# A hybrid DeltaNet and diffusion layer: a written TensorE order for the projections and the DeltaNet pairs, and two modulation blocks as float32 products

## The chip, the cores and the metric

The kernel runs on one core of a Trainium2 chip. The metric is the device time of one execution in microseconds (us); where several runs are compared, it is their median. Engines are named as follows: TensorE (PE in the rows, PEld its weight loads), VectorE (DVE), ScalarE (ACT), GpSimd (POOL), and SyncE (SP), which issues most transfers. All matrices are float32; a product of two of them is made of three one-pass products of a high and a low part (h and l in the tile names), unless the text calls it a float32 product.

## What is computed

One layer of a network for 128 context and 512 latent tokens (640 in all, width 1024). The reference, cut to the part that the change touches:

```python
def layer(x, mod, s0, ...):
    sh1, sc1, gt1, sh2, sc2, gt2 = jnp.split(mod[:, None, :], 6, axis=-1)   # mod = silu(c) @ w_mod + b_mod
    h = rms_norm(x, norm_gains[0]) * (1 + sc1) + sh1
    y, s_fin = mixing(h, s0, ...)
    x = x + gt1 * rms_norm(y, norm_gains[1])
    h = rms_norm(x, norm_gains[2]) * (1 + sc2) + sh2                         # the two blocks sh2, sc2
    gate, up = jnp.split(h @ w_ffn_in, 2, axis=-1)
    ...
def mixing(h, s0, ...):
    p = h @ w_in                                        # 45 tiles of 128 columns
    qkv, z, beta, a, sc, gates = jnp.split(p, SPLITS, axis=-1)
    qkv = jax.nn.silu(conv_centred(qkv, conv_qkv, n_rows))
    o_f, s_f = gated_delta_chunked(q, k, v, beta[0], g[0], s0[:, 0])         # and backwards
    ...
def gated_delta_chunked(q, k, v, beta, g, s0):          # chunks of 64 tokens
    lower = jnp.where(tri_strict, jnp.einsum('bhncd,bhned->bhnce', kb, k) * decay, 0.0)
    tmat = lax.linalg.triangular_solve(eye + lower, ...)                     # 64x64 per chunk and head
    ...
    def step(s, xs):                                    # the scan over the chunks
        v_new = u_c - jnp.einsum('bhcd,bhde->bhce', w_c, s)
        o = jnp.einsum('bhcd,bhde->bhce', q_c, s) + jnp.einsum('bhce,bhed->bhcd', a_c, v_new)
        s = s * jnp.exp(gl)[..., None, None] + jnp.einsum('bhcd,bhce->bhde', k_c, v_new)
        return s, o
```

## The kernel before, in words

The layer runs in stages: norm and modulation of the input, which gives hT (channels on partitions, all 640 tokens in one row); the projections of hT with the 45 tiles of w_in, with the DeltaNet beside them; the merge of the two branches; the output product; the feed-forward part. The change lies in the second of these stages.

A projection tile is 128 columns of w_in. `load_w` fetches its 512 KB into a wr buffer (two of them), ScalarE and VectorE split it into wh and wl in two halves, and `gemm_cm` multiplies it with one half of the tokens (320 columns): 24 products, three for each of eight blocks of the inner dimension, into one of three PSUM buffers named d. Each half is then taken out by ScalarE or VectorE. The tiles belong to q, k and v of four head pairs (`qkv`, with a convolution of three taps on VectorE and a Silu), to the gate z (`zgate`), to the short convolution branch (`short`, three tiles each) and to the merge gates (`gate_th`).

For each head pair, `prepare` turns q, k and v into token-major form (transposes on TensorE), normalises them, multiplies keys with keys and queries (the K products, from kqT), and solves a unit triangle: Md is transposed by 32x32 blocks on VectorE into blk, 30 steps of two instructions (otmp, then X) invert 128 blocks of 32 rows at once, and two transposes give RT and R. TensorE's products with RT and em give Y, and those of R and Y the rest of the 64x64 inverse. Then the tiles KU, RS, AQ and kt are filled for `scan`, which runs eight steps over the chunks, both directions and heads at once; each step is a few small products (EW, then KU) and two copies of the state into RS. Output products (AQ) and five transposes end a pair.

Every engine runs its instructions in the order in which they stand in the program. A scheduler set this order before: each instruction has a priority from its place in the code, raised within `high_priority` (state steps of `scan` by 300000, evacuations by 400000, splits by 200000, `prepare` by 1000), and the scheduler deals them out by its own estimate of when each can start. Buffers are given out in turn; an instruction that writes a buffer waits until the last reader of what was in it has ended.

The modulation blocks sh2 and sc2 are made on VectorE by `row_job`: for each of eight blocks of 128 input channels, w_mod (512 KB) is multiplied by one number per partition and added to a row sum gacc, once for each of the two conditioning vectors; then `cm_rows` splits the sum, adds it over the partitions with TensorE (a product with ones) and carries the row through DRAM into channel-major form.

## Time and profile before

| what | value |
|---|---|
| median of 3 runs | 1090.03 us (1087.43 to 1094.59) |
| profiled execution, its own time | 1085.44 us |
| its span, first to last instruction | 1083.7 us |
| mean granted TensorE clock in it | 0.981 of 2.4 GHz |
| TensorE busy | 1019.8 us, 94% |
| VectorE busy | 836.9 us, 77% |
| ScalarE busy | 483.2 us, 45% |
| GpSimd busy | 141.9 us, 13% |

The span is the profiled execution as the rows below see it; about 2 us of the execution lie outside it. Busy time is the time in which an engine has at least one instruction in work; products overlap, so a busy TensorE need not be at its peak.

### The profile page before, as it was taken

The page shows a single profiled execution, that of the slowest core. Times are in us where ns is not written, and L with a number is a line of the kernel's source. Part 1 is how long each engine was busy: PE and PEld are TensorE (multiplying, and loading weights), DVE is VectorE, ACT ScalarE, POOL GpSimd, SP SyncE. Part 2 cuts the span into 40 slices and gives each one's busy share as a digit, 9 for nine tenths or more (in the row PEclk, how much of TensorE's full clock was granted, in tenths as well). Part 3 has the DMA queues.
Part 4 walks back from the last instruction along what each step waited for, and adds up shares of the span by engine and source line. Part 5 has one row for each costly group of instructions (what it writes and reads, how often), then busy time and mean ns, then how long its engine had stood idle before and what let it go on. Part 6 is the DMA issues. An engine that isn't in the chain of part 4 may idle for free.

```text
span 1083.7 us, 19694 instructions
## 1 busy us (share of the span) xinstructions
PE 1019.8 (94%) x7729; PEld 925.9 (85%) x7729; DVE 836.9 (77%) x1698; ACT 483.2 (45%) x927; POOL 141.9 (13%) x168
## 2 busy tenths in 40 slices
PE   6999988988988989999998998999999999999997
PEld 3699987878887788899996887999999999788885
DVE  5767997897898888895895789888777775975336
ACT  5568436415525323434223476444445444624321
POOL 2215321153063050101000000000000000000000
PEclk9999989998999999999999998999999999999999
DMA  9335712163282374557853532323222322552214
GB/s 346 144 91 136 205 60 75 57 138 107 62 188 89 99 179 166 173 166 241 309 183 116 180 113 88 104 86 98 93 79 78 98 83 74 176 171 99 79 39 156
DMA packets 47399, 141.52 MB, mean 131 GB/s; under 512 B 9517, under 2 KB 10034, under 8 KB 47306
## 3 DMA queue, kind: packets, MB, share of 16 engines
q1 hardware_dynamic: 42746, 127.10, 35.9%
q0 software_dynamic: 4560, 13.15, 5.6%
q8 instruction: 61, 1.00, 0.4%
q14 instruction: 32, 0.26, 0.1%
HBM read 117.57 MB, written 12.18 MB: 120 GB/s over the span
## 4 chain that ended last, share of the span: by engine, by line
PE 63%; DVE 18%; DMA 3%; ACT 2%; issue 2%; SPq 1%; POOL 0%; DVEq 0%; ACTq 0%; POOLq 0%
PE acc L1166 21%; PE d L85 6%; PE d L83 6%; PE d L84 6%; PE acc L84 5%; PE acc L83 5%; PE acc L85 5%; PE d L1166 3%; DVE X L561 3%; DVE otmp L559 2%; PE s L643 2%; DVE wl L58 2%; PE v L614 1%; PE v L673 1%; DVE RT L565 1%
## 5 line engine op out<-in xcount | busy, mean ns | idle before, releaser
L83 PE MATMUL d<-hT,wh 128*128 128x320 f32 x720 | 228.4, 318 | 1.8 <-DVE cy L724 1.8
L85 PE MATMUL d<-hT,wl 128*128 128x320 f32 x720 | 228.9, 318 | 0.4 <-DVE wl L58 0.4
L84 PE MATMUL d<-hT,wh 128*128 128x320 f32 x720 | 227.2, 316 | 0.0
L57 ACT CAST wh<-wr 128x512 fp32r<-128x512 f32 x150 | 88.1, 620 | 155.1 <-PE d L84 90.4
L83 PEld LDWEIGHTS d<-hT,wh 128*128 128x128 f32 x720 | 137.3, 191 | 4.3 <-DVE cy L724 2.1
L85 PEld LDWEIGHTS d<-hT,wl 128*128 128x128 f32 x720 | 137.3, 191 | 4.2 <-issue 1.2
L84 PEld LDWEIGHTS d<-hT,wh 128*128 128x128 f32 x720 | 137.5, 191 | 2.0 <-issue 0.3
L58 DVE TENSOR_TENSOR wl<-wr,wh 128x512 fp32r<-128x512 f32 x150 | 103.1, 709 | 44.3 <-ACT wh L57 43.5
L1166 PE MATMUL acc<-mh,wl 128*128 128x320 f32 x280 | 86.9, 310 | 1.8 <-DVE wl L1101 1.8
L83 PE MATMUL acc<-wh,as 128*128 128x512 f32 x220 | 85.7, 390 | 2.1 <-ACT as L1300 2.1
L1166 PE MATMUL acc<-mh,wh 128*128 128x320 f32 x280 | 87.0, 311 | 0.3 <-ACT early L1180 0.3
L1166 PE MATMUL acc<-ml,wh 128*128 128x320 f32 x280 | 86.7, 310 | 0.0
L84 PE MATMUL acc<-wl,as 128*128 128x512 f32 x220 | 85.6, 389 | 0.0
L85 PE MATMUL acc<-wh,as 128*128 128x512 f32 x220 | 85.5, 389 | 0.0
L196 DVE SCALAR_TENSOR_TENSOR gacc<-wr,cv,gacc 128x1024 f32<-128x1024 f32 x64 | 80.7, 1280 | 4.0 <-DMA wr<-in_w_mod_dram 3.7
L1105 ACT CAST wh<-wr 128x512 fp32r<-128x512 f32 x66 | 40.7, 623 | 71.6 <-PE acc L1166 36.9
L1105 ACT CAST wh<-S 128x512 fp32r<-128x512 f32 x88 | 54.3, 621 | 36.3 <-PE d L1166 19.6
L1101 DVE TENSOR_TENSOR wl<-S,wh 128x512 fp32r<-128x512 f32 x88 | 60.2, 688 | 3.8 <-ACT wh L1105 2.9
L1101 DVE TENSOR_TENSOR wl<-wr,wh 128x512 fp32r<-128x512 f32 x66 | 45.4, 690 | 19.1 <-ACT wh L1105 18.1
L1166 PEld LDWEIGHTS acc<-mh,wl 128*128 128x128 f32 x280 | 52.8, 189 | 2.1 <-DVE wl L1101 2.0
L1166 PEld LDWEIGHTS acc<-mh,wh 128*128 128x128 f32 x280 | 52.7, 188 | 0.6 <-ACT early L1180 0.6
L1166 PEld LDWEIGHTS acc<-ml,wh 128*128 128x128 f32 x280 | 52.8, 189 | 0.0
(365 smaller groups left out, 2344.0 us busy)
## 6 DMA issues: line engine op xcount, KB each, us to landing
wr<-in_w_ffn_in_dram SPq DMA_DIRECT2D x48, 512.0 KB
wr<-in_w_in_dram SPq DMA_DIRECT2D x45, 512.0 KB
wr<-in_w_mod_dram SPq DMA_DIRECT2D x32, 512.0 KB
wr<-in_w_ffn_out_dram SPq DMA_DIRECT2D x22, 512.0 KB
mr<-in_w_mod_dram SPq DMA_DIRECT2D x16, 512.0 KB
thd<-gt SPq DMA_DIRECT2D x16, 320.0 KB
bth<-thd SPq DMA_DIRECT2D x16, 320.0 KB
wr<-in_w_br_dram SPq DMA_DIRECT2D x8, 512.0 KB
```

Of the source, the lines that this page charges most:

```text
L57: (high or nc.scalar.copy)(out=hi[:, s], in_=raw[:, s])
L58: (low or nc.vector).tensor_tensor(out=lo[:, s], in0=raw[:, s], in1=hi[:, s].bitcast(F32), op=ALU.subtract)
L83: mm(out, lhsT=ah, rhs=bh, start=start, stop=False)
L84: mm(out, lhsT=ah, rhs=bl, start=False, stop=False)
L85: mm(out, lhsT=al, rhs=bh, start=False, stop=stop)
L196: nc.vector.scalar_tensor_tensor(out=acc[v], in0=w, scalar=self.cv[:, k, v:v + 1], in1=acc[v], op0=ALU.mult, op1=ALU.add)
L559: nc.vector.tensor_tensor(out=t, in0=B[:, j + 1:32, j:j + 1].broadcast_to([P, n, j]), in1=X[:, j:j + 1, 0:j].broadcast_to([P, n, j]), op=A ...
L561: nc.vector.tensor_tensor(out=X[:, j + 1:32, 0:j], in0=X[:, j + 1:32, 0:j], in1=t, op=ALU.subtract)
L643: mm(ps[half(c2), o:o + 64], lhsT=w(d, c2, t, hd), rhs=R[:, d, c2, t, hd, :], start=True, stop=True)
L1101: tt = lambda o, a, b, op: nc.vector.tensor_tensor(out=o, in0=a, in1=b, op=op)
L1105: nc.scalar.copy(out=dst[0], in_=src)
L1166: nc.tensor.matmul(ps, lhsT=A[x][:, k], rhs=B[y][:, k], start=start and k == 0 and n == 0, stop=k == 3 and n == 2, skip_group_check=True)
```

## The change

Inside the stage, TensorE's instructions are no longer placed by the scheduler: within `manual_schedule` they stand as the code issues them. The other engines are still scheduled. The code is cut into steps with `yield`. `jobs` lists the projection tiles and, as two jobs "m", the modulation blocks 3 and 4 (sh2 and sc2); each step of a job is a quarter of a projection tile (half the inner dimension of one token half, 12 products) or, for "m", two float32 products of a 128x512 piece of w_mod. After each step, two chains are offered a turn: all of `scan` and all of `prepare`, for the four pairs one after the other. What a chain yields is how many turns it lets pass before its next step; a condition beside it holds the count until it is true.

`prepare` is put in another order (em, ea and qtT are fetched at its start, the tiles KU, RS and AQ are filled after the solve and only once the scan of the pair before has issued its output products), `mod_job` replaces `row_job` and `cm_rows` for two blocks, and some copies move from VectorE to ScalarE. Cut to its core:

```diff
+    def gemm_steps(self, w, xT, half):
+        sl = slice(half * HALF, (half + 1) * HALF)
+        ps = self.psd.tile([P, 512], F32, name="d", tag="d")[:, 0:HALF]
+        for k in range(KT):
+            self.mm3(ps, w[0][:, k, :], w[1][:, k, :], xT[0][:, k, sl], xT[1][:, k, sl],
+                     k == 0, k == KT - 1)
+            if k == KT // 2 - 1:
+                yield
         return ps
...
+    def mod_job(self, blk, out):
+        for h in range(2):
+            hs = slice(h * 512, (h + 1) * 512)
+            row = self.da.tile([5, 512], F32, name="mrow")
+            nc.sync.dma_start(out=row[4:5, :], in_=self.I["b_mod"][blk, :, hs])
+            ps = self.psd.tile([P, 512], F32, name="d", tag="d")
+            for kk in range(KT // 2):
+                w = self.wpool.tile([P, 2, 512], F32, name="wr", tag="wr")
+                nc.sync.dma_start(out=w, in_=self.I["w_mod"][blk - 2, 2 * kk:2 * kk + 2, :, hs].rearrange("k p c -> p k c"))
                 for i in range(2):
+                    k = 2 * kk + i
+                    nc.tensor.matmul(ps[0:4, :], lhsT=self.cz[:, k, :], rhs=w[:, i], start=k == 0, stop=k == KT - 1)
+                if kk == KT // 2 - 1:
+                    with self.urgent():
+                        nc.scalar.copy(out=row[0:4, :], in_=ps[0:4, :])
                 yield
+            self.cm_finish(out)(h, row)
...
+    def prepare(self, p, scanned):
...
         for j in (1, 0, 2):
+            yield 2 if j == 1 else 1, lambda: (p, j) in self.cm
...
+        for j, x in enumerate((kh, qh)):
+            yield 5 - 4 * j
...
         for ts in (slice(0, 4), slice(4, 5)):
+            yield 2
...
         for c2, b, s in quad:
-            cp = (nc.vector.tensor_copy, nc.scalar.copy)[b]
-            cp(out=Md[s, 0:20], in_=emv[s, :, b * 32:b * 32 + 32])
+            nc.scalar.copy(out=Md[s, 0:20], in_=emv[s, :, b * 32:b * 32 + 32])
...
+        yield 16
+        pw = self.psw.tile([P, 1024], F32, name="w", tag="w")
         Y = dn.tile([P, 20, 32], F32, name="Y")
...
+        yield 1, lambda: scanned() >= p
...
+        yield 2
+        pw = self.psw.tile([P, 1024], F32, name="w", tag="w")
         quads = [(c2, slice(c2 * 64, c2 * 64 + 32), slice(c2 * 64 + 32, c2 * 64 + 64)) for c2 in range(2)]
...
+    def scan(self, p):
+        yield 4, lambda: p in self.pre
...
-        cp = (nc.scalar.copy, nc.vector.tensor_copy)
+        cp = (nc.scalar.copy, nc.scalar.copy)
         for s_ in range(8):
...
+            yield 1
             if s_ == 7:
                 continue
...
+        self.scans = p + 1
+        yield 5
...
-        self.da = Tags(da, {"t25": 4})
+        self.da = Tags(da, {"t25": 2})
...
+        job = {"q": self.qkv, "z": self.zgate, "s": self.short, "g": self.gate_th,
+               "m": lambda blk, hT: self.mod_job(blk, cm[("sh2", "sc2")[blk - 3]])}
+        qkv = lambda p: [("q", p, j) for j in (1, 0, 2)]
+        jobs = (qkv(0) + [("z", 0), ("g", 0), ("s", 0)] + qkv(1) + [("z", 1), ("m", 3), ("g", 1), ("g", 2)]
+                + qkv(2) + [("z", 2), ("m", 4), ("s", 1)] + qkv(3) + [("z", 3), ("g", 3), ("g", 4), ("s", 2), ("g", 5)]
+                + [("s", 3)] + [("g", i) for i in range(6, 16)])
...
+            def tick(c):
+                if c.ready and not c.ready():
+                    return
+                c.ready = None
+                c.wait -= 1
+                if c.wait <= 0:
+                    c.step()
...
+        with tc.manual_schedule(engines={mybir.EngineType.PE}):
+            scan = Chain((x for p in range(NPAIR) for x in self.scan(p)), 300000)
+            prep = Chain((x for p in range(NPAIR) for x in self.prepare(p, lambda: self.scans)), 1000)
+            running = (x for n, *i in jobs for x in job[n](*i, hT))
+            used = 0
+            while not (scan.done and prep.done):
+                used += next(running, 1) is None
+                scan.tick()
+                prep.tick()
+            for _ in running:
+                pass
...
-        fill = itertools.chain(*(self.row_job(blk, rows2(mb), raws(mb, 4), self.cm_rows(cm[n], mb, ma, parts))
-                                 for blk, n in ((3, "sh2"), (4, "sc2"))))
-        steps = lambda n: [next(fill, None) for _ in range(n)]
-        self.gate_th(3, hT)
-        steps(2)
```

Three places of the order show it. In the rows, the d products with hT and wh or wl are projection products, w with kqT the K products, w or v with RT and em the first products that read the solved triangle.

TensorE, pair 0, from the last K product to the first product with RT; the new program, where 192 projection products stand between the two:

```order
L504 MATMUL w<-kqT 64x128 x4
L83 MATMUL d<-hT_75,wh 128x320
L84 MATMUL d<-hT_76,wh 128x320
L85 MATMUL d<-hT_75,wl 128x320
...
L542 MATMUL w<-RT,em 32x32 x40
```

The program before, where 255 stand there:

```order
L532 MATMUL w<-kqT 64x128 x4
L85 MATMUL d<-hT_75,wl 128x320
L83 MATMUL d<-hT_75,wh 128x320
L84 MATMUL d<-hT_76,wh 128x320
...
L578 MATMUL v<-RT,em 32x32 x40
```

So 63 projection products have left this place for later ones; in the new program the first product with RT comes after exactly four tiles.

VectorE, pair 0, the head of the triangular solve (blk, X and otmp are its tiles; wl is a split of a weight tile, bv and ss belong to the next pair's keys and values); before:

```order
L549 COPY Md<-em 32x640 x2
L553 STREAM_TRANSPOSE blk<-Md 128x32x32
L554 TENSOR_SCALAR X<-blk 128x1024
L555 MEMSET X 128x32
L559 TENSOR_TENSOR otmp<-blk,X 128x30
L561 TENSOR_TENSOR X<-X,otmp 128x30
L559 TENSOR_TENSOR otmp<-blk,X 128x58
L561 TENSOR_TENSOR X<-X,otmp 128x29x2
L559 TENSOR_TENSOR otmp<-blk,X 128x84
L58 TENSOR_TENSOR wl<-wr,wh 128x512 x2
L561 TENSOR_TENSOR X<-X,otmp 128x28x3
L468 TENSOR_TENSOR bv<-tk,beta 128x640
```

And now:

```order
L520 STREAM_TRANSPOSE blk<-Md 128x32x32
L58 TENSOR_TENSOR wl<-wr,wh 128x512 x2
L521 TENSOR_SCALAR X<-blk 128x1024
L522 MEMSET X 128x32
L526 TENSOR_TENSOR otmp<-blk,X 128x30
L528 TENSOR_TENSOR X<-X,otmp 128x30
L526 TENSOR_TENSOR otmp<-blk,X 128x58
L528 TENSOR_TENSOR X<-X,otmp 128x29x2
L730 TENSOR_TENSOR cx<-cx,d 128x320
L526 TENSOR_TENSOR otmp<-blk,X 128x84
L528 TENSOR_TENSOR X<-X,otmp 128x28x3
```

The copies of Md have gone to ScalarE, and the steps of the next pair's keys and values to a later place; splits and steps of the projections stand between those of the solve, as before.

TensorE, the stretch between RT of pair 0 and the last K product of pair 1, where the scan of pair 0 begins; before:

```order
L643 MATMUL s<-RS,EW 64x64
L83 MATMUL d<-hT_75,wh 128x320
L84 MATMUL d<-hT_76,wh 128x320
L85 MATMUL d<-hT_75,wl 128x320
L614 MATMUL v<-EW,kt 64x64 x20
L83 MATMUL d<-hT_75,wh 128x320
L84 MATMUL d<-hT_76,wh 128x320
L532 MATMUL w<-kqT 64x128 x4
```

And now (d with wr and cz are the float32 products of the modulation block, d with selb and mrow its row transposes):

```order
L178 MATMUL d<-wr,cz 4x512 x2
L651 MATMUL s<-RS,EW 64x64 x8
L178 MATMUL d<-wr,cz 4x512 x2
L651 MATMUL s<-RS,KU 64x64 x8
L487 MATMUL w<-ident,kh 128x128 x5
L178 MATMUL d<-wr,cz 4x512 x2
L651 MATMUL s<-RS,EW 64x64 x8
L487 MATMUL w<-ident,tk 128x128 x5
L178 MATMUL d<-wr,cz 4x512 x2
L651 MATMUL s<-RS,KU 64x64 x8
L192 MATMUL d<-selb,mrow 128x2 x4
```

Where projection products stood between the scan steps, two float32 products stand now, each pair of them on a freshly loaded piece of w_mod.

## Rows read from the trace of the kernel before

**Rows 1.** The page: busy time, share of the span and instructions of each engine.

```profile
PE 1019.8 (94%) x7729; PEld 925.9 (85%) x7729; DVE 836.9 (77%) x1698; ACT 483.2 (45%) x927; POOL 141.9 (13%) x168
```

**Rows 2.** Windows: length, busy time and instructions by engine, clock, DMA share, GB/s.

```profile
42.30:116.50 74.20, 71.63 (x542) 68.60 (x543) 54.72 (x120) 51.99 (x82) 28.95 (x29) 1.00 0.46 119
116.50:164.90 48.40, 42.34 (x285) 41.30 (x280) 46.55 (x117) 20.07 (x34) 11.36 (x10) 0.93 0.42 122
184.70:246.70 62.00, 54.62 (x510) 48.52 (x507) 57.24 (x147) 20.95 (x45) 17.98 (x23) 0.97 0.42 104
276.40:330.80 54.40, 47.66 (x436) 43.17 (x432) 50.84 (x140) 18.76 (x41) 18.91 (x23) 1.00 0.56 135
357.40:403.40 46.00, 41.41 (x387) 36.63 (x379) 40.89 (x108) 13.31 (x33) 16.45 (x22) 0.96 0.52 124
403.40:515.60 112.20, 110.66 (x1089) 103.05 (x1090) 88.45 (x125) 45.51 (x93) 9.51 (x12) 1.00 0.59 192
sum 397.20, PE 368.32 PEld 341.27 DVE 338.68 ACT 170.59 POOL 103.16; mean PE 61.39 PEld 56.88 DVE 56.45 ACT 28.43 POOL 17.19
```

**Rows 3.** The same windows, only instructions that touch hT.

```profile
42.30:116.50 74.20, 63.85 (x410) 60.14 (x409) 3.69 (x5) 4.49 (x8) 1.00 0.46 119
116.50:164.90 48.40, 39.97 (x255) 38.80 (x255) 0.00 (x0) 0.00 (x0) 0.93 0.42 122
184.70:246.70 62.00, 42.09 (x246) 36.27 (x246) 0.00 (x0) 0.00 (x0) 0.97 0.42 104
276.40:330.80 54.40, 38.33 (x233) 34.30 (x233) 0.00 (x0) 0.00 (x0) 1.00 0.56 135
357.40:403.40 46.00, 33.20 (x190) 28.79 (x190) 0.00 (x0) 0.00 (x0) 0.96 0.52 124
403.40:515.60 112.20, 94.94 (x594) 88.33 (x594) 0.00 (x0) 0.00 (x0) 1.00 0.59 192
```

**Rows 4.** Windows between RT and the next K, their sum.

```profile
sum 76.10, PE 69.45 PEld 63.08 DVE 57.22 ACT 47.98 POOL 21.90; mean PE 23.15 PEld 21.03 DVE 19.07 ACT 15.99 POOL 7.30
```

**Rows 5.** Waits of TensorE in the stage: total, times, longest.

```profile
PE v L578 <- DVE RT L565: 6.0, 4, 2.3
```

**Rows 6.** Timeline of TensorE, first stage: start, length, instruction.

```profile
33.54 5.31 PE L790 MATMUL m<-mr,cz 128*4 128x512 f32 x12
...
39.12 1.05 PE L180 MATMUL n<-selb,mrow 5*128 5x2 f32 x8
```

**Rows 7.** Timeline of TensorE, two projection products in a row.

```profile
272.90 0.31 PE L83 MATMUL d<-hT,wh 128*128 128x320 f32 x1
273.05 0.31 PE L84 MATMUL d<-hT,wh 128*128 128x320 f32 x1
```

**Rows 8.** Groups of VectorE in the stage: busy us, mean ns, idle before.

```profile
L58 DVE TENSOR_TENSOR wl<-wr,wh 128x512 fp32r<-128x512 f32 x92 | 65.1, 721 | 17.8 <-ACT wh L57 17.2
L561 DVE TENSOR_TENSOR X<-X,otmp 128x30 f32<-128x30 f32 (+14 forms) x120 | 47.8, 398 | 2.2
L559 DVE TENSOR_TENSOR otmp<-blk,X 128x30 f32<-128x30 f32 (+14 forms) x120 | 45.6, 380 | 2.4
L196 DVE SCALAR_TENSOR_TENSOR gacc<-wr,cv,gacc 128x1024 f32<-128x1024 f32 x34 | 42.9, 1278 | 0.1
L379 DVE SCALAR_TENSOR_TENSOR cm<-d,taps,cm 128x315 f32<-128x315 f32 x24 | 13.0, 541 | 9.4 <-ACT cm L401 9.3
...
L565 DVE STREAM_TRANSPOSE RT<-X 128x1024 f32<-128x1024 f32 x4 | 7.8, 1941 | 0.1
```

**Rows 9.** Groups of ScalarE in the stage.

```profile
L549 ACT COPY Md<-em 32x640 f32<-32x640 f32 x8 | 5.8, 726 | 2.3 <-DVE em L537 2.2
```

**Rows 10.** Timeline of VectorE, inside the solve of pair 1.

```profile
224.81 0.39 DVE L559 TENSOR_TENSOR otmp<-blk,X 128x228 f32<-128x228 f32 x1
225.11 0.17 DVE L679 TENSOR_SCALAR so<-so 128x10 f32<-128x10 f32 x1
```

**Rows 11.** Chain that ended last, near the scan of pair 1.

```profile
253.46 4.59 DMA wr<-in_w_in_dram
```

More of the change, by code (lines that the diff above doesn't have):

```diff
@@ L416, in prepare @@
+        half = lambda c2: slice(c2 * 64, c2 * 64 + 64)
+        qtT = dn.tile([P, 2, TOK], F32, name="qtT")
+        for hd in range(2):
+            nc.sync.dma_start(out=qtT[half(hd)], in_=g["scre"][:, 2 * p + hd].unsqueeze(0).broadcast_to([64, 2, TOK]))
         tok = {}
+        ss = dn.tile([P, 2, NT * 2], F32, name="ss")
         for j in (1, 0, 2):
+            yield 2 if j == 1 else 1, lambda: (p, j) in self.cm
+            cm = self.cm.pop((p, j))
             pw = self.psw.tile([P, 1024], F32, name="w", tag="w")
@@ L441, in prepare @@
+        qh, k, v = (tok[j] for j in range(3))
         fac = dn.tile([P, 2, 2, NT, 2], F32, name="fac")
@@ new lines, in prepare @@
+        nc.scalar.activation(out=em, in_=em, func=AF.Exp)
+        nc.scalar.activation(out=ea, in_=ea, func=AF.Exp)
+        kqT = dn.tile([P, 2, TOK], F32, name="kqT", tag="kb")
+        for j, x in enumerate((kh, qh)):
+            yield 5 - 4 * j
+            pw = self.psw.tile([P, 1024], F32, name="w", tag="w")
+            for t in range(NT):
+                nc.tensor.transpose(pw[:, t * P:(t + 1) * P], x[:, t * P:(t + 1) * P], self.ident)
+            nc.scalar.copy(out=kqT[:, j, :], in_=pw[:, 0:TOK])
@@ new lines, in prepare @@
+        RT = dn.tile([P, 32, 32], F32, name="RT", tag="kb")
+        R = dn.tile([P, 32, 32], F32, name="R")
+        nc.vector.transpose(out=RT.rearrange("p m x -> p x m"), in_=X)
+        nc.vector.transpose(out=R.rearrange("p m x -> p x m"), in_=X.rearrange("q r x -> q x r"))
+        yield 16
+        pw = self.psw.tile([P, 1024], F32, name="w", tag="w")
+        Y = dn.tile([P, 20, 32], F32, name="Y")
+        for m in range(20):
+            for c2 in range(2):
+                s0 = slice(c2 * 64, c2 * 64 + 32)
+                s1 = slice(c2 * 64 + 32, c2 * 64 + 64)
+                mm(pw[s0, m * 32:m * 32 + 32], lhsT=emv[s1, m, 0:32], rhs=RT[s1, m, :], start=True, stop=True,
+                   tile_position=(c2 * 64 + 32, c2 * 64))
@@ L899, in run @@
[L899 to L914 removed]
+        self.pre, self.cm, self.scans = {}, {}, 0
@@ new lines, in run, with __init__, step @@
+        class Chain:
+            def __init__(c, gen, offset):
+                c.gen, c.offset = gen, offset
+                c.step()
+            def step(c):
+                with tc.high_priority(offset=c.offset):
+                    w = next(c.gen, None)
+                c.wait, c.ready = (1 << 30, None) if w is None else w if isinstance(w, tuple) else (w, None)
+                c.done = w is None
+            def tick(c):
[4 more added lines that the diff above has]
+                if c.wait <= 0:
+                    c.step()
```

343 lines of the change are left out of this document (115 added, 228 removed).

## Prediction

> **What bounds the kernel now.** I read the page first. TensorE is busy for 94% of the span, VectorE for 77% [rows 1]; that is an average, and the change touches one stage, the 473 us in which TensorE multiplies the normalised input hT with 45 weight tiles and carries the DeltaNet work of four head pairs beside it. So I cut this stage into windows at two TensorE instructions of each pair p: the last key-query product of prepare (K for short) and the first product that reads the solved triangle RT. Between K and RT lies the triangular solve, 60 dependent VectorE steps, and TensorE cannot pass RT until it is done.
>
> The windows [rows 2] are, in this order: the start up to K of pair 0; K to RT of pairs 0, 1, 2, 3; RT of pair 3 to the end. The same windows for instructions that touch hT [rows 3] have as their PE count the number of projection products in each; the three stretches from one pair's RT to the next pair's K are added up [rows 4]. Two things are to be seen. In the four solve windows VectorE is busy 46.6 of 48.4, 57.2 of 62.0, 50.8 of 54.4 and 40.9 of 46.0 us: these 210.8 us go at VectorE's pace, and what TensorE does there (255, 246, 233 and 190 projection products) is filling. Outside them VectorE is busy 57 of 76 us between the pairs and 88 of 112 at the end, where TensorE is busy 69 and 111: these go at TensorE's pace. TensorE's idle time in the whole stage is small, 28.9 us in the six windows and 6.6 in the three; the wait for RT, 6.0 us in four times, is the one that a solve ends [rows 5].
>
> **Units.** One projection product starts 0.147 us after the one before [rows 7], so a quarter tile of twelve is 1.76 us. A float32 product of a 128x512 block on four rows counts as two in the trace; twelve of them took 5.31 us, so one whole product costs 0.885 us, and four small transposes of a modulation row 1.05 us [rows 6].
>
> **The change, part by part.** The stage's work on TensorE hardly shrinks. Added are 32 float32 products (28.3 us) and four times 1.05 us; removed are sixteen one-pass sums of 512 columns, by that pitch 0.235 us each, 3.8 us. Net +29 us. Removed from VectorE are 32 steps of 1.28 us on gacc [rows 8] with eight splits of their sums, and all state copies of scan and half those of Md go to ScalarE. The gacc steps stand in the last window, where TensorE is the one that is late: taking them off gives nothing by itself. So the question is whether the written order fills TensorE better. I go through the windows as the new order sets them.
>
> Start to K of pair 0: 312 products stand there instead of 410, 45.7 us instead of 60.1. The rest of TensorE's time, 74.2 less 60.1 less 2.6 idle, is 11.5 us and stays. New are waits: the transposes of q and of v of pair 0 stand directly behind their own last product, with ScalarE's tap and two VectorE taps of the convolution (0.54 us each [rows 8]), the Silu and the semaphores between. I take 3 us for each and 1 for gates; nothing and 14 us are the ends. 64 us, so 10 less.
>
> K to RT: now 192, 180, 192 and 192 products stand there, 168 fewer in all. The chain is VectorE's. First a lead: the last products with em and four copies of Md, now all on ScalarE at 0.73 us [rows 9] (two of four were on VectorE), 3.9 us. Then VectorE's own row of instructions from the transpose blk up to RT, which I counted in the new order: 92, 97, 102 and 96 instructions. In each 60 are the solve (30 at 0.380, 30 at 0.398: 23.3 us) and 8 are splits of the four weight tiles that TensorE needs meanwhile (5.8 us), the two big transposes at either end are 2.0 each, and the rest convolution, normalisation and short-branch steps; at the mean of their form they add up to 43.8, 42.7, 45.7 and 43.1 us. The form means [rows 8] contain the few steps that GpSimd held up. They overstate in one way: a short step starts before the one ahead has ended (the 0.39 us step at 224.81 has 0.09 us left when the next starts [rows 10]). I take 93% of the lists, 163 us, and four leads, 178.6 us; between 85% and 100% lie 165 and 191. That is 32 less than 210.8. TensorE's own work there is 28 us for pair 0 and about 37 for each other pair (27 us of products, the last scan steps, the output products, in pairs 1 and 2 the end of a modulation block), so it will stand at RT for about 16 us in pair 0 and 7 to 9 in each other, some 40 us where 6.0 are now.
>
> The Trainium skill, VectorE: DVE Perf Modes, in The DRAIN you can't avoid, says that the next VectorE instruction does not start until the pipe of the one ahead is empty. By that the lists count in full, 191 us, and the sum below would be 12 us more. That overlap speaks against it for these short steps, so I keep 93%.
>
> RT to the next K: 120, 108 and 216 products, 444 where 232 stand now, 65.0 us. 30 of the 32 float32 products are here with two of the four row transposes: 28.7 us. The small products of the pairs: in the windows K to RT and RT to K together TensorE now spends 286.9 us, of which 169.4 are products and 31 idle, so 86 go to small products, to changes between the two kinds and to the slower clock; the solve windows of the new order keep 24 of that, 62 would be left. The order changes kinds less often (88 unbroken runs of projection products where there were 129), and the slower clock's share is at least 7 us (one less the clock column, times the window [rows 2]). I take 46, ends 40 and 62. Then the loads. Both kinds of weights come in 512 KB pieces through the same two wr buffers. A projection tile needs one piece per 7 us; a modulation block needs one per tick, and each waits until TensorE has left the piece before last. One piece took 4.59 us to land [rows 11]. With 1.8 us of products that is 6.4 us for two ticks, where TensorE has 5.7 us of work (products, scan and key steps). 0.35 us a tick, 14 ticks: 5 us; nothing and 20 are the ends. TensorE's clock is slow for a while where it has stood idle: the solve window of pair 0 shows 0.93 over 48.4 us now, 3.4 us lost [rows 2]. I take half of that, 1.7, behind each wait at RT; three of the four count here: 5 us. Sum 150 us, against 76.1: 74 more.
>
> RT of pair 3 to the end: 648 products instead of 594, +7.9; the sums go, -3.8; idle time of 1.5 goes; one slow stretch. +3 us. That the scan of pair 3 runs beside them costs nothing as long as a quarter tile of 1.76 us covers the two short copies between two scan steps.
>
> Sum: -10, -32, +74, +3: 35 us more. The profiled execution took 1085.44 us, so 1120; the median of the runs before lies 0.4% above it, so **1125 us** for the median. In one sentence: 168 products leave the stretches in which VectorE needs 45 us anyway and move to stretches where TensorE is the one that is late, and 29 us of new products come on top.
>
> **The rivals.** *The waits vanish (faster).* The order does what it is written for: every chain step is ready at its turn. Then only TensorE's work counts: 57 + 138 + 140 + 115 = 450 us where 473 are now, 1062 in a profile and 1067 as a median. For it speaks that two chains stand at fixed distances; against it that sixteen ticks are 28 us and the 60 steps of the solve alone 23, with the three 2 us transposes, the copies and the splits on top. It decides from the point where the lists run at under 75% of their sum.
> *No change.* The solve's list goes at 85%, loads and transposes are in time: waits of some 20 to 35 us come back and eat the 23. 1085 to 1100. For it speaks that GpSimd holds VectorE up less if its work falls into other stretches.
> *The modulation loads starve (slower still).* A piece takes 8 us because the pieces meet the GpSimd queue's copies of KU, RS and AQ of the next pair, and the loads of em stand between them on SP's queue. (8 + 1.8) less 5.7 is 4.1 us for two ticks, seven times: 29 us on top of the forecast's 5, and the first projection tile behind waits too. 1150.
> That the order isn't what the text says can be excluded: TensorE's row was read from the built program.
>
> **How the numbers follow.** A measurement of this kernel can tell about 1%. Forecast 0.66 (own range 1103 to 1145), waits vanish 0.07, no change 0.14, loads starve 0.13. Faster by over 1% is the first rival alone, 0.07; within 1% is no change and a little of the forecast, 0.15; slower 0.78. The range leaves out the first rival, half of no change and the upper half of the last: 1090 to 1150, which also takes in the ends of the solve's list (13 us either way) and of the loads (15 more).
>
> **What would show it.** The wait of TensorE for RT: four waits, the longest in pair 0 above 10 us, together above 30. K to RT near 45 us in each pair; RT to the next K near 50. In the modulation blocks waits of TensorE for wr, below 3 us each. VectorE busy for some 70 us less in the whole, ScalarE for 25 more, and neither of it in the time. The clock column slow just behind each RT. If the waits at RT are below 5 us each, the list is mis-sized and the forecast falls by as much; if VectorE is idle inside K to RT, another engine (ScalarE's casts, which wait for a piece) sets the solve's pace.

## The result and the profile after

| | before | changed |
|---|---|---|
| median of 4 runs (before: the three above and one more), us | 1088.73 (1086.07 to 1094.59) | 1161.69 (1159.86 to 1164.45) |
| ratio, 95% interval | | 1.0664 [1.0615, 1.0714] |
| span of the profiled execution, us | 1083.7 | 1159.8 |
| first to last product with hT in it, us | 473.3 | 550.4 |

The change costs 73 us; 35 were forecast, and the range ended at 1150. The stage alone grew by 77 us, what lies outside it not at all. The first part of the page (busy time of each engine), to be read beside [rows 1]:

```profile
PE 1059.5 (91%) x7809; PEld 946.9 (82%) x7809; DVE 761.0 (66%) x1578; ACT 503.3 (43%) x997; POOL 134.6 (12%) x156
```

VectorE is busy for 76 us less and TensorE for 40 more; the span grew by 76, so TensorE also stands more. The windows of [rows 2], cut at the same instructions of the changed kernel:

```profile
42.70:126.80 84.10, 66.76 (x443) 62.63 (x445) 44.35 (x98) 38.30 (x65) 29.99 (x29) 0.82 0.36 98
126.80:171.10 44.30, 28.95 (x201) 28.29 (x201) 39.78 (x97) 13.99 (x22) 8.25 (x7) 0.90 0.41 111
219.80:266.30 46.50, 39.56 (x349) 34.71 (x345) 40.25 (x104) 18.34 (x43) 14.76 (x20) 0.96 0.66 166
316.10:366.40 50.30, 39.50 (x359) 35.93 (x354) 44.27 (x112) 17.81 (x43) 14.68 (x20) 0.94 0.59 148
429.80:476.90 47.10, 38.59 (x343) 35.85 (x339) 40.06 (x101) 14.10 (x35) 16.85 (x22) 0.92 0.48 116
476.90:593.10 116.20, 116.20 (x1126) 111.21 (x1127) 45.83 (x66) 45.47 (x102) 0.00 (x0) 0.97 0.50 168
```

And the three windows from RT to the next K, which answer to the sum of [rows 4]:

```profile
171.10:219.80 48.70, 47.45 (x547) 34.27 (x549) 21.31 (x45) 26.40 (x52) 7.62 (x5) 0.95 0.28 90
266.30:316.10 49.80, 46.91 (x541) 32.67 (x541) 22.77 (x46) 30.77 (x55) 12.37 (x10) 0.97 0.41 116
366.40:429.80 63.40, 54.30 (x613) 50.57 (x617) 28.93 (x56) 34.98 (x64) 13.19 (x10) 0.86 0.20 61
sum 161.90, PE 148.66 PEld 117.51 DVE 73.01 ACT 92.16 POOL 33.18; mean PE 49.55 PEld 39.17 DVE 24.34 ACT 30.72 POOL 11.06
```

Beside the forecast:

| windows | before | forecast | measured | off by |
|---|---|---|---|---|
| start to K of pair 0 | 74.2 | 64 | 84.1 | +20 |
| K to RT, four | 210.8 | 178.6 | 188.2 | +10 |
| RT to next K, three | 76.1 | 150 | 161.9 | +12 |
| RT of pair 3 to the end | 112.2 | 115 | 116.2 | +1 |

The clock column is the second thing to see. It is below 1.00 in every window. The whole stage, before and after:

```profile
42.30:515.60 473.30, 437.77 (x4416) 404.34 (x4415) 395.90 (x834) 218.57 (x403) 125.06 (x135) 0.97 0.46 131
42.70:593.10 550.40, 478.23 (x4495) 426.12 (x4494) 327.54 (x721) 240.16 (x474) 117.71 (x123) 0.92 0.43 122
```

In the trace 88.7 us of the stage pass at 1.2 GHz where it was 23.9 before, idle time included. What TensorE waits for in the stage (total, times, longest), where [rows 5] had 6.0 us at RT:

```profile
PE w L431 <- ACT cm L397: 15.0, 3, 5.0
PE w L542 <- DVE RT L532: 14.7, 3, 7.4
PE w L542 <- issue: 14.2, 1, 14.2
PE v L699 <- DVE ob L693: 9.0, 3, 4.1
PE w L431 <- ACT tk L433: 5.4, 2, 4.2
PE w L316 <- DVE g L306: 2.8, 1, 2.8
PE w L431 <- DVE rsb L353: 2.7, 1, 2.7
PE s L651 <- issue: 2.1, 1, 2.1
PE d L178 <- DMA wr<-in_w_mod_dram: 1.7, 2, 1.0
```

The second and third rows are the waits at RT, 28.9 us. The third is that of pair 0 (the trace names no releaser for it; RT of that pair ends 0.1 us earlier); the second is 3.0, 7.4 and 4.4 us in the other pairs. They had been forecast. The first row and the fifth to seventh had not, or not at this size: transposes of q, k and v (L431) and the products of the gates (L316). The start shows how they work. TensorE there, by the timeline (start, length, instruction, idle before):

```profile
60.94 0.31 PE L85 MATMUL d<-hT,wl 128*128 128x320 f32 x1
64.02 0.62 PE L316 MATMUL w<-g,tri 128*128 128x40 f32 x2 [2.77 <-DVE g L306]
...
66.95 0.66 PE L335 MATMUL w<-g,ones 64*64 64x40 f32 x8 [1.04 <-ACT eT L327]
...
75.17 1.30 PE L431 MATMUL w<-ident,cm 128*128 128x128 f32 x5 [2.70 <-DVE rsb L353]
76.12 0.62 PE L83 MATMUL d<-hT,wh 128*128 128x320 f32 x1
```

From 60.94 to 76.12 not one projection product starts. The first transposes of pair 0 are written behind five quarter tiles; they need the one buffer w, which the products of the gates hold in turn, and no later projection product may pass them. In the old order the scheduler had put 28 products between those of the gates.

### The profile page after: what moved, and what is told of

The parts are those of the page before. It is cut to its first block, busy times and chain, and to the rows that moved or that the text cites. A ratio compares the mean times of both kernels' runs of the same rounds, so it can differ in the third digit from the quotient of the medians.

```text
span 1159.8 us, 19735 instructions
## 1 busy us (share of the span) xinstructions
PE 1059.5 (91%) x7809; PEld 946.9 (82%) x7809; DVE 761.0 (66%) x1578; ACT 503.3 (43%) x997; POOL 134.6 (12%) x156
## 4 chain that ended last, share of the span: by engine, by line
PE 54%; issue 25%; DVE 15%; ACT 3%; DMA 2%; POOL 1%; SPq 0%; DVEq 0%; ACTq 0%; POOLq 0%
PE acc L1150 19%; PE acc L83 4%; PE acc L85 4%; PE acc L84 4%; PE d L83 4%; PE d L85 4%; PE d L84 3%; PE d L1150 3%; DVE X L528 2%; DVE otmp L526 2%; PE d L178 2%; DVE wl L58 2%; PE s L651 1%; PE m L807 1%; PE w L431 1%
## 5 line engine op out<-in xcount | busy, mean ns | idle before, releaser
L83 PE MATMUL d<-hT,wh 128*128 128x320 f32 x720 | 239.7, 334 | 2.1 <-DVE cy L739 1.2
L84 PE MATMUL d<-hT,wh 128*128 128x320 f32 x720 | 229.8, 320 | 0.0
L83 PEld LDWEIGHTS d<-hT,wh 128*128 128x128 f32 x720 | 142.8, 198 | 7.1 <-DVE cy L739 1.5
L85 PEld LDWEIGHTS d<-hT,wl 128*128 128x128 f32 x720 | 142.2, 198 | 1.5 <-DVE wl L58 1.5
L84 PEld LDWEIGHTS d<-hT,wh 128*128 128x128 f32 x720 | 142.8, 199 | 0.0
L1085 DVE TENSOR_TENSOR wl<-wr,wh 128x512 fp32r<-128x512 f32 x66 | 45.3, 689 | 18.3 <-ACT wh L1089 17.3
L208 DVE SCALAR_TENSOR_TENSOR gacc<-wr,cv,gacc 128x1024 f32<-128x1024 f32 x32 | 39.9, 1281 | 21.1 <-DMA wr<-in_w_mod_dram 18.9
```

The source lines that it names most:

```text
L83: mm(out, lhsT=ah, rhs=bh, start=start, stop=False)
L84: mm(out, lhsT=ah, rhs=bl, start=False, stop=False)
L85: mm(out, lhsT=al, rhs=bh, start=False, stop=stop)
L208: nc.vector.scalar_tensor_tensor(out=acc[v], in0=w, scalar=self.cv[:, k, v:v + 1], in1=acc[v], op0=ALU.mult, op1=ALU.add)
L1085: tt = lambda o, a, b, op: nc.vector.tensor_tensor(out=o, in0=a, in1=b, op=op)
```

## The experiments

"Stage" is the time from the first to the last product with hT in the trace. Each time is a median with its lowest and highest run; the ratio is against the kernel before, run beside it, whose medians lay between 1086.87 and 1089.44 us. Where two of these runs are compared with each other, it is their medians.

### Theories

**Mine, after the result:** about 28 us of the 73 are the products of the blocks; the rest is TensorE standing at a few written places, at RT and (the part that I had too small) at the gates and transposes, together with the lower clock behind each. **Rivals:** the blocks cost much more than their products; or the rewriting beside the order (ScalarE's copies, fewer buffers, later filling of KU, RS and AQ) costs.

### The start: three turns more

```diff
-            yield 2 if j == 1 else 1, lambda: (p, j) in self.cm
+            yield 3 * (2 if j == 1 else 1) if p == 0 else 2 if j == 1 else 1, lambda: (p, j) in self.cm
```

> One edit: the three transposes of pair 0 (of k, q and v) come three times as many turns behind the moment at which they are offered, so that 36 more projection products stand ahead of the last K product of pair 0 and the products of the gates can be spread among projection products, instead of standing behind each other while the one w buffer is handed on. Theory (the start is long because TensorE stands before small products that have nothing beside them, and its clock drops there): TensorE's idle time from the start to K of pair 0 falls from 17.3 to below 4 us, the clock there from 0.82 to above 0.95, and the window takes 64 to 70 us with 348 products, where it took 84.1 with 312; in all 17 to 24 us less than the changed kernel, 1138 to 1145. Rival (K of pair 0 is set by the steps on VectorE and ScalarE, and TensorE's waits only show it): the window keeps its length of 84 us or grows by the three turns, and the time stays within 5 us of 1162.

The three distances of pair 0 are tripled; its last K product comes three quarter tiles later by it. 1145.60 us (1142.98 to 1148.57), 1.0531 [1.0499, 1.0563]: 16 us less than the changed kernel, just short of what was expected. Its windows start to K of pair 0 and RT of pair 2 to K of pair 3:

```profile
42.70:114.40 71.70, 64.44 (x483) 61.96 (x481) 47.62 (x100) 43.62 (x71) 30.93 (x30) 0.95 0.43 121
364.30:416.60 52.30, 49.33 (x597) 45.85 (x597) 27.01 (x52) 34.15 (x62) 13.79 (x10) 0.90 0.24 75
```

71.7 us with 348 products is 12.4 less than 84.1 with 312, and 36 products are worth 5.3 more: 17.7 us won in this window, nearly all of the 20 by which it had missed the forecast, with the clock at 0.95 for 0.82. The idle time fell from 17.3 to 7.3 us, not below 4 as expected. The second row was no aim: three turns of shift took the transposes of pair 3 off their waits as well, 63.4 to 52.3 us with 12 products less. Two windows between got longer by 5 us each. The rival, that VectorE and ScalarE set K of pair 0, falls.

### Blocks and order apart

The two blocks back on VectorE, in the written order (the row sums start when pair 3 is prepared):

```diff
-        jobs = (qkv(0) + [("z", 0), ("g", 0), ("s", 0)] + qkv(1) + [("z", 1), ("m", 3), ("g", 1), ("g", 2)]
-                + qkv(2) + [("z", 2), ("m", 4), ("s", 1)] + qkv(3) + [("z", 3), ("g", 3), ("g", 4), ("s", 2), ("g", 5)]
+        jobs = (qkv(0) + [("z", 0), ("g", 0), ("s", 0)] + qkv(1) + [("z", 1), ("g", 1), ("g", 2)]
+                + qkv(2) + [("z", 2), ("s", 1)] + qkv(3) + [("z", 3), ("g", 3), ("g", 4), ("s", 2), ("g", 5)]
...
+            fill = itertools.chain(*(self.row_job(blk, rows2(mb), raws(mb, 4), self.cm_rows(cm[n], mb, ma, parts), 3)
+                                     for blk, n in ((3, "sh2"), (4, "sc2"))))
...
+                if i % 2:
+                    next(fill, None)
```

> The two modulation blocks go back to VectorE (row sums beside the last stretch, started when the preparation of pair 3 is done), all else as in the changed kernel, the written order with its distances too; the sixteen turns of the blocks are gone. Theory (the blocks cost what their products cost, since TensorE sets the pace between the pairs): 28 us of products less, 4 us of one-pass sums more, and 0 to 5 for the end of the row sums: 20 to 27 us less, 1135 to 1142. Rival A (the blocks cost more than their products, by loads and by the slower clock behind them): 40 us or more less, below 1122. Rival B (the turns with blocks filled waits that are there anyway): less than 10 us less, above 1152.

1149.19 us (1148.19 to 1151.61): between the theory (1135 to 1142) and rival B (above 1152). But the stage had lost 33 us (517.3), and the first product of the merge then waited 14.0 us for its weights. With the row sums twice as dense:

> The run with the blocks back on VectorE, with the row sums issued twice as densely, so that they end earlier: there the stage itself got 34 us shorter, but the first product of the merge then waited 14 us for its weights. Theory (that wait is the late end of the row sums, which hold the memory that the merge's weights go to): it goes to below 3 us and 10 to 14 us come back, 1135 to 1140; the stage stays 30 to 35 us shorter than the changed kernel's. Rival (the merge waits for its own loads and splits): the wait stays above 10 us, 1147 to 1151.

1131.51 us (1130.63 to 1137.00), 1.0414 [1.0372, 1.0455]: the wait went from 14.0 to 4.8 us, the stage takes 510.3, and the whole is better than the theory had it: 30 us less than the changed kernel.

The blocks alone in the kernel before, under the scheduler:

```diff
-        fill = itertools.chain(*(self.row_job(blk, rows2(mb), raws(mb, 4), self.cm_rows(cm[n], mb, ma, parts))
-                                 for blk, n in ((3, "sh2"), (4, "sc2"))))
+        fill = itertools.chain(*(self.mod_job(blk, cm[n], mb) for blk, n in ((3, "sh2"), (4, "sc2"))))
```

> The kernel before with one edit: the two modulation blocks as float32 products, 32 of them, each half a block summed in one PSUM buffer, at the same places in the code as the row sums had (the last stretch), with four buffers for the pieces; the order stays the scheduler's. Theory (TensorE is the one that is late there, so its 28.3 us and 4.2 of transposes come on top, less 3.8 of sums, and the 41 us that VectorE loses were cover): 24 to 30 us more than the kernel before, 1113 to 1120. Rival (VectorE's relief gives a part back): 0 to 12 us more, 1090 to 1102.

1173.93 us (1169.85 to 1174.80): 87 us more, outside both. The window of that run from RT of pair 2 to RT of pair 3, instructions that touch hT:

```profile
329.10:393.80 64.70, 0.00 (x0) 0.00 (x0) 0.00 (x0) 0.00 (x0) 0.53 0.30 67
```

No projection product at all, and the clock at 0.53. By the program the sum of a block takes a d buffer in turn, but its pieces go to memory that is freed only behind the preparation of pair 3; so the tiles behind it, which had filled these windows, could not run ahead. In the trace no projection product starts between 311.6 and 413.5 us. The first product of a block starts at 408.4, and from 413.5 the three tiles that stand behind it in the code follow with all six halves, while the sum of the block is still open. So it is the turn that kept them back, and not a lack of free buffers. With PSUM buffers of its own (`ps = ma()` in place of the d tile):

> The run with the blocks alone, mended: there the sums of the blocks held one of the three d buffers from their place in the code on, and the projection products behind it in the buffer's turn could not go ahead; for 65 us between pair 2 and pair 3 not one ran. Now the blocks sum in two PSUM buffers of their own, as the row sums did. Theory (TensorE is the one that is late in the last stretch, so the blocks cost their products): 24 to 30 us more than the kernel before, 1111 to 1118. Rival (VectorE's relief gives a part back): 0 to 12 us more, 1087 to 1099.

1117.83 us (1115.13 to 1122.12), 1.0276 [1.0239, 1.0313]: 31 us more, at the upper end of the theory, and 56 less than with the d buffers. The rival, that VectorE's relief of 41 us gives a part back, falls: in the stretch where TensorE is late, the blocks cost their products.

The order given back to the scheduler, all else changed:

```diff
-        with tc.manual_schedule(engines={mybir.EngineType.PE}):
+        with nullcontext():
```

> The changed kernel with TensorE's order given back to the scheduler in this stage; code, turns, copies on ScalarE and modulation blocks as they are. Theory (about 28 us of the 73 are the blocks, the rest the written places at which TensorE stands): the scheduler fills the waits at RT and in the start, so 30 to 45 us less, 1115 to 1130. Rival (what was rewritten beside the order costs as much: fewer buffers, the copies on ScalarE, filling KU, RS and AQ behind the scan of the pair before): 1145 to 1165.

1109.62 us (1109.52 to 1110.74), 1.0202 [1.0177, 1.0227]: 52 us less, more than my theory had it. The three windows RT to K of this run:

```profile
160.70:199.10 38.40, 37.18 (x538) 22.14 (x538) 20.36 (x39) 27.16 (x63) 8.63 (x6) 0.96 0.42 132
244.90:282.20 37.30, 36.73 (x542) 22.62 (x542) 16.78 (x35) 24.98 (x59) 9.22 (x7) 0.95 0.31 92
337.90:375.60 37.70, 37.04 (x582) 31.98 (x582) 26.47 (x51) 30.04 (x65) 8.44 (x6) 0.95 0.16 50
sum 113.40, PE 110.95 PEld 76.74 DVE 63.60 ACT 82.18 POOL 26.29; mean PE 36.98 PEld 25.58 DVE 21.20 ACT 27.39 POOL 8.76
```

127 projection products stand here where the written order has 444; the others lie under the solves (239, 258, 233 and 239, where the written order has 756 in all), in the start (385) and in the last stretch (679). The start, and the sum of the start and the four solve windows:

```profile
42.40:116.50 74.10, 71.02 (x516) 67.87 (x518) 48.57 (x102) 43.81 (x72) 27.25 (x27) 0.95 0.40 113
sum 262.00, PE 234.99 PEld 221.99 DVE 212.70 ACT 111.60 POOL 89.41; mean PE 47.00 PEld 44.40 DVE 42.54 ACT 22.32 POOL 17.88
```

So the four solve windows take 187.9 us with 969 products, and they take 188.2 with 756 in the written order: the 213 products more do not lengthen them. The written order loses 48.5 us between RT and the next K and 10 in the start; the last stretch gives 6 back.

Both parts undone:

> The changed kernel without its two parts: TensorE's order given back to the scheduler and the blocks back on VectorE; what stays is the rest of the rewriting (code in turns of quarter tiles, copies of Md and of the states on ScalarE, KU, RS and AQ filled behind the scan of the pair before, loads of em and ea at the head). Theory (the two parts add up: the blocks cost 31 us in the kernel before, the written order 52): 1109.6 less 28 to 31, 1078 to 1082, faster than the kernel before by some 0.6%. Rival (the rest of the rewriting is worth nothing or costs): 1085 to 1095.

1098.20 us (1096.57 to 1102.76), 1.0088 [1.0067, 1.0109]: 3 us above the rival's 1085 to 1095, and far from the theory. The stage takes 472.4 us, as before the change; behind the stage the profiled execution loses 15 us, and 9.7 of them are one wait at the merge for its weights, of the kind that the denser row sums shortened above (the other 5 stay open). So the rest of the rewriting, taken together, is worth nothing and costs nothing in the stage. My sum failed mainly because undoing the blocks brought a wait with it that the kernel before doesn't have. The stages, with their clock, of the blocks alone, of the blocks back with the written order, of the scheduler's order, and of both undone:

```profile
42.50:545.70 503.20, 467.41 (x4496) 412.36 (x4495) 363.05 (x801) 213.11 (x395) 114.65 (x123) 0.97 0.46 134
42.50:552.80 510.30, 443.24 (x4414) 411.99 (x4412) 359.22 (x748) 234.59 (x472) 128.22 (x135) 0.93 0.41 118
42.40:539.90 497.50, 466.21 (x4496) 412.75 (x4495) 324.38 (x722) 240.98 (x476) 115.71 (x124) 0.97 0.48 135
42.40:514.80 472.40, 448.07 (x4414) 414.61 (x4412) 351.08 (x747) 239.16 (x477) 120.57 (x133) 0.95 0.44 124
```

The six stages together:

| stage, us | blocks on VectorE | blocks on TensorE |
|---|---|---|
| kernel before | 473.3 | 503.2 |
| rewritten, scheduler's order | 472.4 | 497.5 |
| rewritten, written order | 510.3 | 550.4 |

Blocks: 30, 25 and 40 us. Written order: 38 us without them and 53 with. Of the 15 between 25 and 40, most is again order: without the sixteen turns the transposes of pair 3 fall elsewhere, and its window from RT of pair 2 takes 48.2 us with 204 products instead of 63.4 with 216, 13 us apart when the 12 products are taken off. That is read from windows, and the start edit moved the same window by 9 us; it was not tried by itself.

### The waits at RT

```diff
-        yield 16
+        yield (24, 18, 21, 19)[p]
```

> The start edit, and on it one number: 24, 18, 21 and 19 turns for pairs 0 to 3 between the solve and the products with RT, where 16 stood. Against the run with the start edit alone, 1145.6: Theory (TensorE stands at RT because sixteen turns are too few, and the list of VectorE hardly changes): the waits at RT, there 16.1 in pair 0 and 17.0 in the three others, fall below 8 together, less of the stage runs at the slow clock, and 18 quarter tiles of 1.76 us that stood in the last stretch lie under the solve: 22 to 32 us less, 1114 to 1124. Rival (more turns bring more splits and evacuations into VectorE's list, so that RT comes later by as much): the waits fall by less than half, above 1134.

1124.41 us (1123.44 to 1129.93), 1.0343 [1.0307, 1.0380]: 21 us less than the start edit alone, a hair outside the theory's 1114 to 1124. Waits of TensorE in the stage:

```profile
PE d L178 <- DMA wr<-in_w_mod_dram: 18.3, 7, 9.8
...
PE w L542 <- issue: 2.2, 1, 2.2
PE w L542 <- DVE RT L532: 1.5, 1, 1.5
```

33.1 us at RT became 3.7. VectorE's list did not grow: from the start of blk to the end of RT the four pairs take 165.8 us together, 167.9 with the start edit alone. In pairs 1 and 2 RT is now ready 3.3 and 3.6 us before TensorE comes to read it. But a wait of 18.3 us for pieces of w_mod took part of it back: the starving that I had as a rival for the changed kernel, where it is 1.7, comes when the blocks' turns fall otherwise.

The same with the blocks' turns in the last stretch, one after two quarter tiles each (`("x", 3, 7), ("x", 4, 11)` in `jobs`; the job x deals a block among four gate tiles):

> The start edit and the turns of 24, 18, 21 and 19, written order, blocks on TensorE, but their sixteen turns stand in the last stretch, behind RT of pair 3, each after two quarter tiles, and no longer in a row between the pairs. Theory (of the 1124.4 us of the run with start and turns, 18.3 are waits for pieces of the blocks, because there they stand in a row behind longer distances; among quarter tiles a piece has three turns to land): those waits fall below 4 us and the slow stretch behind the longest goes, 1102 to 1112. Rival (the pieces share buffers and queue with the weight tiles, so that the wait only moves to the tiles): waits of TensorE for wr, wh and wl together above 12 us, 1116 or more.

1115.71 us (1114.66 to 1117.77), 1.0244 [1.0211, 1.0277]. The waits for pieces are gone, and those for wh are 8.6 us (two, one of 4.8 in the stage): 9 us won of the 12 to 22 expected. Neither number was met, the rival's 1116 by 0.3 us. The waits went as the theory has it, but not for nothing: the 4.8 us for wh and 5.3 us at transposes for tk are new, and in pairs 2 and 3 RT is ready 8.2 and 9.5 us before TensorE comes to read it, so these distances are too long in this arrangement.

All three edits together, and the blocks on VectorE:

> Three edits on the changed kernel together: the start edit, 24, 18, 21 and 19 turns ahead of RT, and the blocks back on VectorE with the dense row sums. The order stays written. Theory (the written order costs by the few places at which TensorE stands, and these are now mended; the blocks cost their products and, with longer turns, waits for their pieces of 18 us): 1124.4 less 28 to 36, 1088 to 1096, level with the kernel before. Rival (the written order costs in many small places that the scheduler fills): 1100 to 1115.

1108.29 us (1107.17 to 1109.12). This kernel leaves out the end of the scan of pair 3 (56 of 608 scan products) and its output products, since its turns ended with the last projection tile. With them:

> The three edits together again, now with the whole scan of pair 3, of which the run before left out the end, because its turns ended with the last projection tile. Theory (the longer distances and the late start of the row sums have emptied the last stretch: 18 quarter tiles stand there for a scan that wants some 30 turns, and TensorE waits there for row sums and for weights, 15.7 and 17.1 us in the run before): the end of the scan lies partly in those waits, 1108 to 1120, so what was won at RT is in part given back at the end. Rival (the scan's end fits into those waits altogether or the waits were a consequence of its lack): 1088 to 1104.

1114.54 us (1113.42 to 1117.56), 1.0235 [1.0205, 1.0264], as expected. The two largest waits; the longest of each, 13.4 and 14.0 us, lie behind the last projection product:

```profile
PE v L719 <- DVE ob L713: 22.2, 4, 13.4
PE d L83 <- ACT wh L57: 14.0, 1, 14.0
```

The projections end 454 us after their start, 97 us earlier than in the changed kernel, and the end of the scan of pair 3 then runs bare. There is one stock of products to lie beside waits: what the longer distances take for the solves is missing at the end (216 projection products behind RT of pair 3, where 468 stood with sixteen turns). Two other things lengthen that end, and no run separates them: the 14.0 us are again the wait at the merge for its weights, and in pairs 2 and 3 RT is ready 8.0 and 4.1 us before TensorE comes to read it. A written order with its distances set anew for the blocks on VectorE was not run. No written order that I ran beats the scheduler's, and no version here beats the kernel before.

### The clock by itself

```diff
+    def dummies(self, n):
+        ps = self.pss.tile([P, 512], F32, name="s", tag="s")
+        for i in range(n):
+            k = i % KT
+            self.nc.tensor.matmul(ps[:, 0:HALF], lhsT=self.hT[0][:, k, 0:P], rhs=self.hT[0][:, k, 0:HALF], start=True, stop=True)
...
+            if p == 0 and j != 1:
+                self.dummies(30)
...
+        if p == 0:
+            self.dummies(80)
```

> The changed kernel with products added that nobody reads, of one projection block each, into the idle s buffer: 30 ahead of the transposes of q and 30 ahead of those of v of pair 0, and 80 ahead of the first product with RT of pair 0. They lie in waits of 5.0, 5.0 and 14.2 us, so TensorE keeps at work there and goes on at the same moments. Theory (a wait costs more than its length, because TensorE's clock is at its lower level for a while behind it): granted clock 1.00 in the three places where it was 0.5 for 6.8, 6.8 and 13.7 us with 5.4, 3.8 and 4.8 us of work in them, about half of it won: 5 to 8 us less although 140 products are added, 1153 to 1157. Rival (the clock costs nothing that isn't in the waits): 1160 to 1164, or more.

1159.80 us (1155.56 to 1160.96), 1.0651 [1.0617, 1.0685]: the median is 2 us under the changed kernel's, within what the runs differ, so by the times it is open. The profiled execution, the quickest of the four (1155.56 us), shows the mechanism at two of the three places. Three windows (around the waits for q, for v and for RT), first of the changed kernel:

```profile
87.00:94.00 7.00, 5.43 (x22) 5.44 (x23) 2.37 (x4) 6.11 (x7) 4.87 (x4) 0.51 0.29 82
100.80:107.60 6.80, 3.77 (x15) 3.77 (x16) 5.01 (x12) 2.71 (x3) 5.08 (x3) 0.50 0.24 78
160.00:176.00 16.00, 4.91 (x90) 4.87 (x91) 12.10 (x30) 6.59 (x13) 0.00 (x0) 0.57 0.13 43
```

and with the added products:

```profile
87.00:94.00 7.00, 6.66 (x47) 6.66 (x48) 2.25 (x5) 6.59 (x8) 4.70 (x4) 1.00 0.44 117
100.80:107.60 6.80, 6.80 (x49) 6.80 (x48) 4.06 (x3) 1.13 (x2) 6.50 (x5) 1.00 0.01 4
160.00:176.00 16.00, 13.67 (x227) 13.13 (x227) 10.11 (x21) 7.62 (x15) 0.00 (x0) 0.89 0.15 45
```

The clock column is 1.00 in the first two and 0.89 in the third: there the added products end 2.3 us before the products with RT start, the clock is at 1.2 GHz from 166.4 to 169.8 us all the same, and the first projection products behind RT start every 0.267 us as before. From the transposes of q to those of v it is 12.7 us (87.34 to 100.07) where it was 15.3 (88.57 to 103.83); from there to the first K product 15.9 where it was 17.6. 4 us won at two waits of 5 us. At RT the clock was not held where it counts, and what that is worth stays open.

## Why the prediction was wrong

Right were the sign, and the mechanism of each large term:
- **VectorE's list.** 93% of the lists, 163 us, was taken. From the start of blk to the end of RT it is 40.3 us in pair 0 (130.7 to 169.1 + 1.9), 40.2 and 42.0 in pairs 1 and 2 and 42.6 in pair 3, together 165.1, which is 94%:

```profile
L520 DVE STREAM_TRANSPOSE blk<-Md x4: 2077/2098/2129, 130.7 to 434.2; 128x1024 f32<-128x1024 f32 x4
```

```profile
L532 DVE STREAM_TRANSPOSE RT<-X x4: 1907/1908/1910, 169.1 to 474.9; 128x1024 f32<-128x1024 f32 x4
```

  In these four stretches the instructions of VectorE last 173.4 us by their own lengths, and VectorE is busy for 156.6 us: 211 of 383 start before the one ahead has ended. It is idle for the other 8.6 us, which the forecast did not count; the overlap alone makes 89% of the 175.3, so the 93% came out near partly by luck. The rule of the Trainium skill that was weighed against it (VectorE: DVE Perf Modes, The DRAIN you can't avoid) does not hold as a general one for this row of short steps; the same section says that a next instruction that is not held starts earlier, and the rows agree with that. The 191 us that the rule gave for the four windows are near the measured 188.2 only because the lead is longer.
- **Waits at RT**, 14.2 in pair 0 and 28.9 together (16 and some 40 forecast, and above 30 named as the sign; all idle time of the four windows is 41.6). In the other pairs they are 3.0, 7.4 and 4.4 where 7 to 9 were taken: this is not a shorter list; TensorE's work is about 2 us longer in each of these windows, and it waits before that for ob (9.0 us in three times). **Loads of the blocks**, 1.7 us of waits where 5 was taken. **Blocks**, 30 us of the stage by themselves (29 forecast). **Last stretch**, 1 us off. VectorE 76 us less busy (70 forecast), ScalarE 20 more (25).

Wrong were sizes, all in one direction:
1. **"I take 3 us for each and 1 for gates."** This step failed worst. The transposes of q and v waited 5.0 us each, and at the gates 15 us passed without a projection product. I had costed the waits by their releasers and had not asked what may stand beside the gates' small products once the order is fixed: nothing, since the one buffer w ties the first transposes to them. The 20 us are two halves. TensorE is idle for 17.3 us in this window, where 7 were taken; its work takes 66.8 us, where 57.2 were taken (45.7 and 11.5), and 30.7 us of the window are at 1.2 GHz. With the start edit it is idle for 7.3 us, and its work takes 64.4 where the same sum with 348 products gives 62.5: 17.7 of the 20 us came back.
2. **The slower clock, 5 us behind three waits.** The stage has twelve stretches at 1.2 GHz, 3.4 to 17.1 us long, where it had five. In the trace TensorE is at work for 63.5 us of the stage at the lower clock (20.9 before); with a projection product every 0.267 us there and every 0.147 at the higher, the 42.6 us more are worth some 19 us, where I had taken 5 and one stretch in the last window. This is an estimate from the spacing of projection products alone, and it overlaps with the other points (the start's longer work is part of it). Here it is the Trainium skill (TensorE: Matmul & The Clock Gate, HAM oscillation — how this bites in real kernels) that describes it: work that is cut up by waits starts at the lower clock each time anew. The rows agree for the two waits of 5.0 us in the start, with the clock at 0.51 and 0.50 around them; the added products of the last experiment point the same way by 4 us, without the times settling it.
3. **The lead of 3.9 us, four times.** It is 23.1 us instead of 15.6: 4.0, 6.3, 8.3 and 4.5. VectorE waits for ScalarE's copies of Md before blk:

```profile
DVE blk L520 <- ACT Md L516: 8.2, 3, 3.2
```

4. **RT to K of pair 3**: 63.4 us. Its transposes wait as those of pair 0 do (4.2 for tk, 4.9 for cm), which I had costed at pair 0 alone. These 9.1 us are most of the 12 by which the three windows miss. The start edit and the blocks' return to VectorE, which shift that place in the order, took the window to 52.3 and 48.2 us.

So the forecast's last sentence, that products leave places where VectorE needs its time anyway, holds, but its balance was wrong: with 29 us for the blocks it left 6 for the written order, and that costs 38 without the blocks and 53 with them. (In the rival of the starving loads, the 29 us stand in place of the forecast's 5, as its 1150 has it, and not on top of them.)

## What to carry to other kernels

An order written at fixed distances has to be costed at every place where the fixed engine meets a chain, not only at the longest one: list each handover, ask what may still run beside it, and count each wait with the slow clock behind it. Before work is moved onto the engine that is late, ask what the engine that is relieved was bounding there; 41 us off VectorE gave nothing by themselves, and 28 us on TensorE cost 25 to 30 under the scheduler and 40 in the written order. A buffer given out in turn is an order too: a block that is next in turn and cannot start yet can stop work that has nothing to do with it.

## What was not expected of the hardware

The lower clock costs a projection product 0.267 us instead of 0.147, not quite twice. The timeline behind the wait for RT of pair 0 (the clock goes up at about 175.9):

```profile
173.80 0.47 PE L84 MATMUL d<-hT,wh 128*128 128x320 f32 x1
174.07 0.47 PE L85 MATMUL d<-hT,wl 128*128 128x320 f32 x1
```

Products that nobody reads, put into waits of 5 us, shortened what came after them in one profiled execution by 2.5 and 1.7 us; the medians do not settle it.
